# Head products of 64 contraction rows in the two halves of TensorE's array, in place of zero-padded key copies

## The chip, the cores and the metric

The kernel runs on one core of one Trainium2 chip. The metric is the time of one execution on the device in microseconds, as the median of several runs. TensorE (PE) multiplies matrices, VectorE (DVE) and ScalarE work element by element, GpSimd (POOL) does a few small operations, and the queue of SyncE (SP) issues nearly all transfers.

## The reference

The network has two layers of 256 tokens and width 1024. Each layer is a half-step feed-forward part, a mixer, and a second half-step feed-forward part. The mixer works on four groups of four heads with 64 features each, all in float32:

```python
    y_fox = merge_heads(forgetting_attention(to_heads(fq), to_heads(fk), to_heads(fv), fox_logf))
...
    h_m = mlstm_chunkwise(to_heads(mq), to_heads(mk), to_heads(mv),
...
    h_r = chunked_decay_attention(rq, rk, to_heads(rv), ret_loga)
...
    h_s = chunked_decay_attention(Ch, Bh, xh * dt[..., None], dt * A[:, None])
```

Each of the four needs, per head, the products of all queries with all keys no later than they are: a contraction over the 64 features of the head. In ssd (the last) two heads share one key group, so that there are two products instead of four.

## The kernel before

The feed-forward and projection products use pairs of float32r numbers, a high and a low part (`whi`, `wlo`), with three matmuls for each product. The weights come by transfer into `raw`; ScalarE makes the high part (L193) and DVE the low one (L194). Between them DVE works off conditioning sums (L246, `araw`) that have nothing to do with the mixer. These projection matmuls (L660 to L662 and L211 to L213) are what PE does between the steps of the mixer.

In `mixers_in`, run once for each layer, `ORDER` (L49) gives the order in which the parts are traced; a scheduler then puts each engine's instructions in a row, so that PE finds projection matmuls while a mixer waits. What stands in a row on one engine runs in that order.

Queries and keys lie with features on partitions: heads 0 and 1 in the first tile of 128 partitions, 64 each, heads 2 and 3 in the second. A product of one head should take 64 of the 128 rows. The kernel takes all 128 instead: the keys are copied into tiles of zeros (`kz[0]` for retention and later fox, `kz[1]` for mlstm, `bz` for ssd), with each head's 64 rows in their place and zeros in the others. `pad_copy` (L682) writes them in two operations of 64 partitions, from `e_rk` (L1032), `e_mk` (L1065) and `e_fk` (L1084); `e_sbc` writes `bz` in a loop. POOL clears the tiles at the stage's start (L611).

The products come in blocks, each in one PSUM bank of `bank_b`, a pool of three banks. In mlstm (`qk_ts`, L744) and fox (L960) block 0 is the first 128 queries of all four heads, 128 columns each; blocks 1 and 2 are the later 128 queries of two heads each, 256 columns a head. Retention has two blocks of two heads with 256 columns (L995) and one of four with 128 (L1000); ssd has two products of each length (L865, L866). fox adds a row sum with `add_row` (L742) into the same bank first.

Behind the products: DVE multiplies mlstm's scores and sums them in one operation per head (L939), for fox it adds the mask and takes the maximum (L964), and for retention it multiplies by `dec` (L997, L1001). mlstm and fox then transpose the weights on PE (`transpose_p`, L767 to L772; fox only after ScalarE's exponentials, L969), and `pv_tm` (L711, L713) makes the weighted sum of the values in a bank of the same pool, the numerator. `head_norm` squares it on ScalarE (L815) and sums it on DVE (L817); for the power of -0.5 the factor goes through POOL (`rsqrt`, L336 and L337). `scaled` (L1071) multiplies mlstm's numerator by the factor into `ml`; until then its bank is taken. Last, each mixer's output is transposed (`to_fm`, L693) for the output projection.

## Time and profile before

| | |
|---|---|
| median of 3 runs | 1102.37 us (1099.95 to 1106.05) |
| the profiled execution | 1099.75 us, its span 1098.0 us |
| PE, DVE, ScalarE, POOL busy | 98%, 78%, 49%, 5% of the span |
| the two mixing stages | about 212 to 347 us and 752 to 886 us |

A matmul's recorded length includes the way through the array, which overlaps the next matmul; the distance from one start to the next is what a matmul costs in a row. In a timeline a merged row gives the start of its first instruction, the time to the end of its last, and their count. A float32 product is two passes on PE, each recorded as a matmul of its own; a program's listing counts it once.

### The profile page before, as it was taken

To read this page: it belongs to the slowest core of one execution; us is meant where nothing else is said; L and a number is where in the kernel's file an instruction comes from. 1 tells how busy PE (TensorE), PEld (TensorE's weight loads), DVE (VectorE), ACT (ScalarE), POOL (GpSimd) and SP (SyncE) were. 2 spreads that over 40 slices of the span, in tenths; PEclk is the share of its full clock that TensorE was granted. 3 is DMA by queue.
4 is the path that set the end of the run, shared out by engine and by line. 5 is a ranking of instruction groups with operands and counts; after the bars stand their busy time and mean duration, and the time that the engine had idled before them with its cause. 6 is when DMAs were issued, how large, how long until landed. Compare 5 with 4: busy or idle time off the path is not lost.

```text
span 1098.0 us, 21819 instructions
## 1 busy us (share of the span) xinstructions
PE 1075.2 (98%) x8785; PEld 1058.8 (96%) x8785; DVE 859.2 (78%) x1511; ACT 538.1 (49%) x893; POOL 59.2 (5%) x76
## 2 busy tenths in 40 slices
PE   8999999999999999999999999899999999999998
PEld 6999999999999999999999999899999999999998
DVE  6899889799858988788888888886976688666541
ACT  4565434455555654334465434345545567444441
POOL 0000000200012000000100000011001120000010
PEclk9999999999999999999999999899999999999999
DMA  9889889955425688888858888884633355655531
GB/s 366 325 315 344 311 316 339 307 186 200 155 86 173 214 295 295 311 300 318 285 199 287 298 317 294 300 284 157 210 99 116 115 186 189 198 179 189 180 130 39
DMA packets 73879, 258.17 MB, mean 235 GB/s; under 512 B 10161, under 2 KB 12465, under 8 KB 73266
## 3 DMA queue, kind: packets, MB, share of 16 engines
q1 hardware_dynamic: 73490, 256.26, 67.4%
q8 instruction: 69, 1.13, 0.4%
q10 hardware_dynamic: 288, 0.52, 0.1%
q14 instruction: 32, 0.26, 0.1%
HBM read 255.70 MB, written 1.05 MB: 234 GB/s over the span
## 4 chain that ended last, share of the span: by engine, by line
PE 76%; DMA 9%; DVE 8%; issue 4%; ACT 2%; POOL 0%; SPq 0%; DVEq 0%; ACTq 0%; POOLq 0%
PE pa L212 22%; PE pa L213 22%; PE pa L211 21%; DMA araw<-in_ada_dram 7%; DVE wlo L194 3%; PE pa L660 2%; PE pa L661 2%; PE pa L662 2%; DMA raw<-in_w13a_dram 1%; ACT whi L193 1%; PE pb L711 1%; DVE ul L378 1%; DVE araw L246 1%; DMA sh<-in_ada_dram 1%; PE stat L329 1%
## 5 line engine op out<-in xcount | busy, mean ns | idle before, releaser
L193 ACT ACTIVATE whi<-raw 128x1024 fp32r<-128x1024 f32 (+1 forms) x340 | 354.3, 1046 | 270.7 <-issue 75.9
L194 DVE TENSOR_TENSOR wlo<-raw,whi 128x1024 fp32r<-128x1024 f32 (+1 forms) x340 | 411.2, 1213 | 95.7 <-ACT whi L193 95.1
L211 PE MATMUL pa<-hh,whi 128*128 128x256 f32 x1424 | 404.5, 284 | 1.3 <-ACT whi L193 1.3
L213 PE MATMUL pa<-hh,wlo 128*128 128x256 f32 x1424 | 403.2, 283 | 0.5 <-DVE wlo L194 0.5
L212 PE MATMUL pa<-hl,whi 128*128 128x256 f32 x1424 | 403.2, 283 | 0.0
L211 PEld LDWEIGHTS pa<-hh,whi 128*128 128x128 f32 x1424 | 273.2, 192 | 3.5 <-ACT whi L193 2.2
L213 PEld LDWEIGHTS pa<-hh,wlo 128*128 128x128 f32 x1424 | 273.2, 192 | 0.7 <-DVE wlo L194 0.7
L212 PEld LDWEIGHTS pa<-hl,whi 128*128 128x128 f32 x1424 | 273.2, 192 | 0.6 <-issue 0.5
L211 PE MATMUL pa<-sh,whi 128*128 128x256 f32 x704 | 200.9, 285 | 3.8 <-ACT sh L518 3.8
L212 PE MATMUL pa<-sl,whi 128*128 128x256 f32 x704 | 201.1, 286 | 3.2 <-DVE sl L519 3.2
L213 PE MATMUL pa<-sh,wlo 128*128 128x256 f32 x704 | 200.7, 285 | 0.0
L246 DVE CUSTOM_DVE_ANT_0 araw<-araw,cact 128x1024 f32<-128x1024 f32 x128 | 159.3, 1245 | 48.7 <-DMA araw<-in_ada_dram 48.0
L211 PEld LDWEIGHTS pa<-sh,whi 128*128 128x128 f32 x704 | 136.7, 194 | 4.2 <-ACT sh L518 4.2
L212 PEld LDWEIGHTS pa<-sl,whi 128*128 128x128 f32 x704 | 136.8, 194 | 3.6 <-DVE sl L519 3.6
L213 PEld LDWEIGHTS pa<-sh,wlo 128*128 128x128 f32 x704 | 136.8, 194 | 0.0
L518 ACT ACTIVATE sh<-s 128x256 fp32r<-128x256 f32 x88 | 36.1, 411 | 125.3 <-DVE s L511 121.0
L322 POOL TENSOR_TENSOR acc<-acc,sq 128x256 f32<-128x256 f32 x30 | 27.4, 912 | 694.0 <-ACT sq L320 693.7
L212 PE MATMUL pa<-ul,whi 128*128 128x258 f32 x208 | 60.1, 289 | 1.3 <-DVE ul L378 1.3
L211 PE MATMUL pa<-uh,whi 128*128 128x258 f32 x208 | 60.0, 290 | 0.9 <-ACT uh L377 0.9
L213 PE MATMUL pa<-uh,wlo 128*128 128x258 f32 x208 | 60.4, 291 | 0.0
L660 PE MATMUL pa<-whi,hh 128*128 128x256 f32 (+1 forms) x192 | 55.9, 291 | 0.0
L662 PE MATMUL pa<-whi,hl 128*128 128x256 f32 (+1 forms) x192 | 55.6, 290 | 0.0
(262 smaller groups left out, 1328.8 us busy)
## 6 DMA issues: line engine op xcount, KB each, us to landing
araw<-in_ada_dram SPq DMA_DIRECT2D x128, 512.0 KB, 5.2
raw<-in_w13b_dram SPq DMA_DIRECT2D x88, 512.0 KB, 4.6
raw<-in_w13a_dram SPq DMA_DIRECT2D x76, 512.0 KB, 5.7
raw<-in_w2a_dram SPq DMA_DIRECT2D x44, 512.0 KB, 5.2
raw<-in_w2b_dram SPq DMA_DIRECT2D x44, 512.0 KB, 4.2
raw<-in_wfm_dram SPq DMA_DIRECT2D x32, 512.0 KB, 4.8
raw<-in_wtm_dram SPq DMA_DIRECT2D x24, 512.0 KB, 4.4
raw<-in_wo_dram SPq DMA_DIRECT2D x16, 512.0 KB, 3.9
```

The source lines that it names most:

```text
L193: act.activation(out=hi, in_=raw, func=AF.Copy)
L194: dve.tensor_tensor(out=lo, in0=raw, in1=hi.bitcast(F32), op=ALU.subtract)
L211: pe.matmul(o, lhsT=wh, rhs=xh, start=first, stop=False)
L212: pe.matmul(o, lhsT=wh, rhs=xl, start=False, stop=False)
L213: pe.matmul(o, lhsT=wl, rhs=xh, start=False, stop=last)
L246: dve.tensor_tensor_reduce(out=raw, in0=raw, in1=cact, scale=0.5, scalar=0.0, op0=ALU.mult, op1=ALU.add, accum_out=cond[l][:, i:i + 1])
L322: eng.tensor_tensor(out=s.acc, in0=s.acc, in1=sq, op=ALU.add)
L329: m = pe.matmul(s.ps[:, t:t + 1], lhsT=v[:, t * P:(t + 1) * P], rhs=ones[:, 0:1], start=(x == 0 and t == 0), stop=(x == len(vs) - 1 and t ...
L518: act.activation(out=sh[:, c, :], in_=s, func=AF.Copy)
L660: pe.matmul(os[t], lhsT=h[0][:, k, ts], rhs=wh[:, y, :], start=(k == 0), stop=False)
L661: pe.matmul(os[t], lhsT=h[0][:, k, ts], rhs=wl[:, y, :], start=False, stop=False)
L662: pe.matmul(os[t], lhsT=h[1][:, k, ts], rhs=wh[:, y, :], start=False, stop=(k == KT - 1))
```

## The change

The padded tiles, their clearing and `pad_copy` are gone. The keys of retention, mlstm, fox and ssd lie in tiles of their own (`kr`, `km`, `kf`, `bt`) without zeros, each written in one operation of 128 partitions.

A new function, `products`, makes a block of all four heads: for each tile x of two heads, the head in partitions 0 to 63 into bank `os[0]` and the one in 64 to 127 into bank `os[1]`, each with 64 contraction rows. Every one is pinned behind the PE instruction traced before it. A block now takes two banks, and there are two blocks instead of three: 128 columns a head, which fill half of each bank, and 256, which fill them. For retention the 256 come first. DVE's operations go through the heads of one bank and then of the other; retention has four of them instead of three. ssd's products go to two banks, one for each key group.

```diff
@@ -605,10 +605,8 @@
 
     def mixers_in(mp, l, st, done):
         h = []
-        kz = [mp.tile([P, 4, T], F32, name=f"kz{i}") for i in range(2)]
-        bz = mp.tile([P, 2, T], F32, name="bz")
-        for t in kz + [bz]:
-            pool.memset(t, 0.0)
+        kr, km, kf = (mp.tile([P, 2, T], F32, name=f"k{i}") for i in "rmf")
+        bt = mp.tile([P, T], F32, name="bt")
         row = mp.tile([P, NC_ROW], F32, name="row")
         sp.dma_start(out=row, in_=row_in[l].partition_broadcast(P))
         dec = mp.tile([P, 4, T], F32, name="dec")
@@ -679,13 +677,6 @@
                     pool.tensor_tensor(out=v[:, t, :], in0=v[:, t, :], in1=g, op=ALU.mult)
             return v
 
-        def pad_copy(dst, fn):
-
-            for j in range(2):
-                ps = slice(64 * j, 64 * j + 64)
-                n = dst.shape[1] // 2
-                fn(dst.rearrange("p (n j) t -> p j n t", j=2)[ps, j], ps)
-
         def to_fm(y):
             o = bank_b()
             for t in range(2):
@@ -741,15 +732,22 @@
             x = rows[:, :P] if o.shape[-1] == P else rows[:, P:]
             pe.matmul(o, lhsT=selR[:, r:r + 1].to_broadcast([P, P]), rhs=x, start=first, stop=last)
 
-        def qk_ts(q, k, b, o):
-
-            n = P if b == 0 else T
-            tsl = slice(0, P) if b == 0 else slice(P, T)
-            for x, h in enumerate(heads_of(b)):
-                pe.matmul(o[:, x * n:(x + 1) * n], lhsT=q[:, h // 2, tsl], rhs=k[:, h, :n], start=True, stop=True)
-
-        def heads_of(b):
-            return list(range(4)) if b == 0 else [2 * b - 2, 2 * b - 1]
+        def products(os, a, asl, b, bsl, first=True):
+
+
+            n = bsl.stop - bsl.start
+            for x in range(2):
+                for j in range(2):
+                    ps = slice(64 * j, 64 * j + 64)
+                    tc.keep_in_program_order(pe.matmul(os[j][:, x * n:(x + 1) * n], lhsT=a[ps, x, asl], rhs=b[ps, x, bsl],
+                                                       start=first, stop=first or x == 1))
+
+        def half_heads(p, j):
+
+            return p.rearrange("p (a j) t -> p j a t", j=2)[:, j]
+
+
+        BLOCKS = ((slice(0, P), slice(0, P)), (slice(P, T), slice(0, T)))
 
         def p_tiles():
             t = hp.tile([P, KT * TS], F32, tag="u", name="pp", bufs=2)
@@ -860,16 +858,17 @@
                 for x, (oo, lt, rh) in enumerate(mm):
                     pe.matmul(oo, lhsT=lt, rhs=rh, start=(x == 0), stop=(x == len(mm) - 1))
                 act.activation(out=(e1 if b == 0 else e0[:, hs, :]).rearrange("p h t -> p (h t)"), in_=o, func=AF.Exp)
-            o0, o1 = bank_b(), bank_b()
-            for g in range(2):
-                pe.matmul(o0[:, g * T:(g + 1) * T], lhsT=bz[:, g, :P], rhs=sc, start=True, stop=True)
-                pe.matmul(o1[:, g * P:(g + 1) * P], lhsT=bz[:, g, P:], rhs=sc[:, P:], start=True, stop=True)
+            og = bank_b(), bank_b()
+            for ss, n0, n1 in (slice(0, P), 0, T), (slice(P, T), T, T + P):
+                for g in range(2):
+                    ps = slice(64 * g, 64 * g + 64)
+                    pe.matmul(og[g][:, n0:n1], lhsT=bt[ps, ss], rhs=sc[ps, ss.start:], start=True, stop=True)
             for g in range(2):
                 hs = slice(2 * g, 2 * g + 2)
                 dve.tensor_tensor(out=e0[:, hs, :], in0=e0[:, hs, :],
-                                  in1=o0[:, g * T:(g + 1) * T].unsqueeze(1).to_broadcast([P, 2, T]), op=ALU.mult)
+                                  in1=og[g][:, :T].unsqueeze(1).to_broadcast([P, 2, T]), op=ALU.mult)
                 dve.tensor_tensor(out=e1[:, hs, :], in0=e1[:, hs, :],
-                                  in1=o1[:, g * P:(g + 1) * P].unsqueeze(1).to_broadcast([P, 2, P]), op=ALU.mult)
+                                  in1=og[g][:, T:T + P].unsqueeze(1).to_broadcast([P, 2, P]), op=ALU.mult)
             ox = bank_b()
             for t in range(2):
                 for j in range(2):
...
@@ -931,14 +931,15 @@
                 act.activation(out=p0[:, h, :], in_=p0[:, h, :], func=AF.Exp, bias=nm[:, h:h + 1])
                 act.activation(out=p1[:, h, :], in_=p1[:, h, :], func=AF.Exp, bias=nm[:, 4 + h:5 + h])
             den = mp.tile([P, 8], F32, tag="den", name="den")
-            for b in range(3):
-                o = bank_b()
-                qk_ts(mq, kz[1], b, o)
-                for x, h in enumerate(heads_of(b)):
-                    pp, n, d = (p0, P, h) if b == 0 else (p1, T, 4 + h)
-                    dve.tensor_tensor_reduce(out=pp[:, h, :], in0=pp[:, h, :], in1=o[:, x * n:(x + 1) * n],
+            for b, (ts, ss) in enumerate(BLOCKS):
+                os = bank_b(), bank_b()
+                products(os, mq, ts, km, ss)
+                pp, n = (p0, p1)[b], ss.stop
+                for j, h in ((j, 2 * x + j) for j in range(2) for x in range(2)):
+                    x = h // 2
+                    dve.tensor_tensor_reduce(out=pp[:, h, :], in0=pp[:, h, :], in1=os[j][:, x * n:(x + 1) * n],
                                              scale=1.0 / 32, scalar=0.0, op0=ALU.mult, op1=ALU.add,
-                                             accum_out=den[:, d:d + 1])
+                                             accum_out=den[:, 4 * b + h:4 * b + h + 1])
             dve.scalar_tensor_tensor(out=den, in0=den, scalar=-1.0, in1=den, op0=ALU.mult, op1=ALU.max)
             dve.tensor_tensor(out=den, in0=den, in1=em, op=ALU.max)
             dve.reciprocal(out=den, in_=den)
@@ -949,19 +950,16 @@
             p0, p1 = p_tiles()
             m = mp.tile([P, 8], F32, tag="fm", name="fm")
             den = mp.tile([P, 8], F32, tag="fden", name="fden")
-            for b in range(3):
-                o = bank_b()
-                n = P if b == 0 else T
-                tsl = slice(0, P) if b == 0 else slice(P, T)
-                hs = heads_of(b)
-                for x, h in enumerate(hs):
-                    add_row(o[:, x * n:(x + 1) * n], arow, h, x == 0)
-                for x, h in enumerate(hs):
-                    pe.matmul(o[:, x * n:(x + 1) * n], lhsT=fq[:, h // 2, tsl], rhs=kz[0][:, h, :n], start=False,
-                              stop=(x == len(hs) - 1))
-                for x, h in enumerate(heads_of(b)):
-                    pp, n, d, am = (p0, P, h, amask) if b == 0 else (p1, T, 4 + h, amask1)
-                    dve.tensor_tensor_reduce(out=pp[:, h, :], in0=o[:, x * n:(x + 1) * n], in1=am, scale=1.0,
+            for b, (ts, ss) in enumerate(BLOCKS):
+                os = bank_b(), bank_b()
+                pp, n, am = (p0, p1)[b], ss.stop, (amask, amask1)[b]
+                for j in range(2):
+                    for x in range(2):
+                        add_row(os[j][:, x * n:(x + 1) * n], arow, 2 * x + j, x == 0)
+                products(os, fq, ts, kf, ss, first=False)
+                for j, h in ((j, 2 * x + j) for j in range(2) for x in range(2)):
+                    x, d = h // 2, 4 * b + h
+                    dve.tensor_tensor_reduce(out=pp[:, h, :], in0=os[j][:, x * n:(x + 1) * n], in1=am, scale=1.0,
                                              scalar=NEG, op0=ALU.add, op1=ALU.max, accum_out=m[:, d:d + 1])
             dve.tensor_scalar(out=m, in0=m, scalar1=-1.0, scalar2=None, op0=ALU.mult)
             for pp, x in ((p0, 0), (p1, 4)):
@@ -988,17 +986,12 @@
 
         def ret_front(rq, rv):
             p1, p0 = p_tiles()
-            for hb in range(2):
-                o = bank_b()
-                for x in range(2):
-                    h = 2 * hb + x
-                    pe.matmul(o[:, x * T:(x + 1) * T], lhsT=kz[0][:, h, :P], rhs=rq[:, h // 2, :], start=True, stop=True)
-                hs = slice(2 * hb, 2 * hb + 2)
-                dve.tensor_tensor(out=p0[:, hs, :], in0=o.rearrange("p (h t) -> p h t", h=2), in1=dec[:, hs, :], op=ALU.mult)
-            o = bank_b()
-            for h in range(4):
-                pe.matmul(o[:, h * P:(h + 1) * P], lhsT=kz[0][:, h, P:], rhs=rq[:, h // 2, P:], start=True, stop=True)
-            dve.tensor_tensor(out=p1, in0=o.rearrange("p (h t) -> p h t", h=4), in1=dec[:, :, :P], op=ALU.mult)
+            for p, ss in (p0, slice(0, P)), (p1, slice(P, T)):
+                os, n = (bank_b(), bank_b()), T - ss.start
+                products(os, kr, ss, rq, slice(ss.start, T))
+                for j in range(2):
+                    dve.tensor_tensor(out=half_heads(p, j), in0=os[j][:, :2 * n].rearrange("p (a t) -> p a t", a=2),
+                                      in1=half_heads(dec[:, :, :n], j), op=ALU.mult)
             num = pv_tm(p0, p1, rv)
             f = head_norm(num, "r")
             return num, f
@@ -1030,8 +1023,7 @@
             rotary(rotated("rq"), lambda r, rs: dve.tensor_tensor(out=v["rq"], in0=r, in1=rs, op=ALU.add))
 
         def e_rk():
-            rotary(rotated("rk"), lambda r, rs: pad_copy(
-                kz[0], lambda o, ps: dve.tensor_tensor(out=o, in0=r[ps], in1=rs[ps], op=ALU.add)))
+            rotary(rotated("rk"), lambda r, rs: dve.tensor_tensor(out=kr, in0=r, in1=rs, op=ALU.add))
 
         def e_sx():
             th, a = conv_silu(mp, taken("sx", "rl"), l, C_SW, C_SB, (0, 1))
@@ -1042,9 +1034,7 @@
             th, a = conv_silu(mp, taken("sbc", "ml"), l, C_SW, C_SB, (2, 3))
             v["sc"] = mp.tile([P, T], F32, tag="sc", name="sc")
             silu2(v["sc"], th[:, 1, :], a[:, 1, :])
-            for j in range(2):
-                ps = slice(64 * j, 64 * j + 64)
-                silu2(bz[ps, j, :], th[ps, 0, :], a[ps, 0, :])
+            silu2(bt, th[:, 0, :], a[:, 0, :])
 
         def e_v(name):
             v[name] = tm_evac(v["o" + name], "v")
...
```

The lines cut away are the loop headings of mlstm's row sums and the two one-line copies of `km` and `kf`.

PE in layer 0 at mlstm's products, before (`pa` rows are projection matmuls, L767 transposes for head 0):

```order
L661 MATMUL pa<-wlo,hh 128x256
L662 MATMUL pa<-whi,hl 128x256
L749 MATMUL pb<-kz_2674,mq 128x128 x4
L749 MATMUL pb<-kz_2674,mq 128x256 x4
L660 MATMUL pa<-whi,hh 128x256
L661 MATMUL pa<-wlo,hh 128x256
L662 MATMUL pa<-whi,hl 128x256
L660 MATMUL pa<-whi,hh 128x256
L661 MATMUL pa<-wlo,hh 128x256
L767 MATMUL pb<-tab,pp 128x128
```

and with the change, where L742 is the line of `products`, L765 transposes for head 0, and `pa` rows from L658 on are the projection:

```order
L659 MATMUL pa<-wlo,hh 128x256
L742 MATMUL pb<-km,mq 128x128 x4
L742 MATMUL pb<-km,mq 128x256
L660 MATMUL pa<-whi,hl 128x256
L658 MATMUL pa<-whi,hh 128x256
L742 MATMUL pb<-km,mq 128x256 x3
L765 MATMUL pb<-tab,pp 128x128
L659 MATMUL pa<-wlo,hh 128x256
L660 MATMUL pa<-whi,hl 128x256
L658 MATMUL pa<-whi,hh 128x256
```

The second block is cut into one product and three, with two projection matmuls between (three in layer 1), and five more (nine in layer 1) now stand behind the first transpose.

PE in layer 0 from retention's products (`kz_2673`) to its weighted sum (`v,pp`), before:

```order
L995 MATMUL pb<-rq,kz_2673 128x256 x3
L1000 MATMUL pb<-rq,kz_2673 128x128 x4
L661 MATMUL pa<-wlo,hh 128x256
L662 MATMUL pa<-whi,hl 128x256
L660 MATMUL pa<-whi,hh 128x256
L711 MATMUL pb<-v,pp 128x64 x5
L661 MATMUL pa<-wlo,hh 128x256
L713 MATMUL pb<-v,pp 128x64
```

and with the change, from the first product of the block of 128 columns on; ahead of it stand the three products of 256 columns and twelve projection matmuls:

```order
L742 MATMUL pb<-rq,kr 128x128
L660 MATMUL pa<-whi,hl 128x256
L658 MATMUL pa<-whi,hh 128x256
L659 MATMUL pa<-wlo,hh 128x256
L660 MATMUL pa<-whi,hl 128x256
L742 MATMUL pb<-rq,kr 128x128 x3
L658 MATMUL pa<-whi,hh 128x256
L659 MATMUL pa<-wlo,hh 128x256
L660 MATMUL pa<-whi,hl 128x256
L658 MATMUL pa<-whi,hh 128x256
L659 MATMUL pa<-wlo,hh 128x256
L702 MATMUL pb<-v,pp 128x64 x5
```

Between the end of mlstm's weighted sum and retention's there are now 21 projection matmuls, where three stood; in layer 1 there are 16. The one product of 256 columns that comes before them stands inside mlstm's weighted sum, as before.

DVE in layer 0 at retention (`pp<-pb,dec` are the copies of its scores, `hv` the norm factor, `ml` the scaled numerator of mlstm), before:

```order
L997 TENSOR_TENSOR pp<-pb,dec 128x512
L817 TENSOR_REDUCE hv<-hsq 128x8
L997 TENSOR_TENSOR pp<-pb,dec 128x512
L819 TENSOR_TENSOR hv<-hv,den 128x8
L1001 TENSOR_TENSOR pp<-pb,dec 128x512
L820 TENSOR_TENSOR hv<-hv,den 128x8
L246 ISA araw,cond_89<-araw,cact 128x1024
L246 ISA cond_89 128x1
L336 TENSOR_SCALAR hv<-hv 128x8
L823 TENSOR_TENSOR hv<-hv,den 128x8
L817 TENSOR_REDUCE hv<-hsq 128x8
L1071 TENSOR_TENSOR ml<-pb,hv 128x512
```

and with the change:

```order
L815 TENSOR_REDUCE hv<-hsq 128x8
L993 TENSOR_TENSOR pp<-pb,dec 128x2x256
L817 TENSOR_TENSOR hv<-hv,den 128x8
L993 TENSOR_TENSOR pp<-pb,dec 128x2x256
L818 TENSOR_TENSOR hv<-hv,den 128x8
L251 TENSOR_TENSOR cond_89<-cond_89,col 128x8
L336 TENSOR_SCALAR hv<-hv 128x8
L262 SCALAR_TENSOR_TENSOR cond_89<-cond_89,col 128x8
L821 TENSOR_TENSOR hv<-hv,den 128x8
L1061 TENSOR_TENSOR ml<-pb,hv 128x512
L993 TENSOR_TENSOR pp<-pb,dec 128x2x128 x2
L815 TENSOR_REDUCE hv<-hsq 128x8
```

The copies of the 128-column block have moved behind `ml`, and a conditioning sum that stood between now comes earlier.

At fox the first block (four row sums, four products) is followed by two row sums, then ten projection matmuls, and then the two other row sums and the four products of 256 columns; before, the three blocks stood one behind the other. Seventeen projection matmuls come between the last product and the first transpose, as before (sixteen in layer 1 before). ssd's four products stand together, 256 columns twice and then 128 columns twice. Between the transposes of mlstm's output and of ssd's there are 52 projection matmuls, 32 before.

## Rows read from the trace of the kernel before

**Rows 1.** The page's busy table: engine, busy us, share, instructions.

```profile
PE 1075.2 (98%) x8785; PEld 1058.8 (96%) x8785; DVE 859.2 (78%) x1511; ACT 538.1 (49%) x893; POOL 59.2 (5%) x76
```

**Rows 2.** Busy time in the first mixing stage (us from the span's start; busy, instructions, clock).

```profile
212.00:347.00 135.00, 132.38 (x1060) 128.57 (x1059) 109.42 (x258) 70.16 (x131) 13.23 (x16) 1.00 0.50 168
```

**Rows 3.** PE's timeline at ssd's products: start, length us, line, tile, count.

```profile
268.47 0.38 PE L866 MATMUL pb<-sc,bz 128*128 128x128 f32 x2
268.69 0.60 PE L865 MATMUL pb<-sc,bz 128*128 128x256 f32 x2
269.12 0.38 PE L866 MATMUL pb<-sc,bz 128*128 128x128 f32 x2
```

**Rows 4.** PE's timeline at the conditioning rows (strips of columns).

```profile
10.03 0.25 PE L329 MATMUL stat<-tab,acc 128*128 128x1 f32 x1
...
10.21 1.04 PE L268 MATMUL pb<-raw,ck 128*1 128x256 f32 x16
11.18 0.73 PE L166 MATMUL pa<-warm 128*128 128x512 f32 x2
```

**Rows 5.** The operation that writes mlstm's padded copies: ns least/median/most, first and last start.

```profile
L598 DVE SCALAR_TENSOR_TENSOR kz<-cvt,cva x4: 673/687/690, 278.1 to 816.7; 64x512 f32<-64x512 f32 x4
```

**Rows 6.** Timeline of PE and DVE at mlstm's products, layer 0.

```profile
288.00 0.28 PE L662 MATMUL pa<-whi,hl 128*128 128x256 f32 x1
288.12 2.78 PE L749 MATMUL pb<-kz,mq 128*128 128x128 f32 x16
...
287.80 2.48 DVE L194 TENSOR_TENSOR wlo<-raw,whi 128x1024 fp32r<-128x1024 f32 x2
290.19 0.28 DVE L939 CUSTOM_DVE_ANT_0 pp<-pp,pb 128x128 f32<-128x128 f32 x1
```

**Rows 7.** Timeline of PE, ScalarE and DVE at retention, layer 0; in brackets idle and releaser.

```profile
297.34 1.51 PE L995 MATMUL pb<-rq,kz 128*128 128x256 f32 x6
...
300.12 1.22 PE L711 MATMUL pb<-v,pp 128*128 128x64 f32 x10
...
297.54 0.60 ACT L815 ACTIVATE hsq<-pb 128x512 f32<-128x512 f32 x1 [2.68 <-PE pb L713]
...
298.02 0.69 DVE L997 TENSOR_TENSOR pp<-pb,dec 128x512 f32<-128x512 f32 x1 [2.88 <-PE pb L995]
298.63 0.67 DVE L817 TENSOR_REDUCE hv<-hsq 128x8 f32<-128x512 f32 x1
299.23 0.68 DVE L997 TENSOR_TENSOR pp<-pb,dec 128x512 f32<-128x512 f32 x1
...
301.79 0.17 DVE L336 TENSOR_SCALAR hv<-hv 128x8 f32<-128x8 f32 x1
303.71 0.17 DVE L823 TENSOR_TENSOR hv<-hv,den 128x8 f32<-128x8 f32 x1 [1.75 <-POOL hv L337]
...
304.39 0.68 DVE L1071 TENSOR_TENSOR ml<-pb,hv 128x512 f32<-128x512 f32 x1
```

**Rows 8.** Timeline of PE and DVE at fox, layers 0 and 1.

```profile
308.60 0.48 PE L742 MATMUL pb<-rows,selR 128*128 128x256 f32 x2
...
311.66 0.28 DVE L964 CUSTOM_DVE_ANT_0 pp<-pb,tab 128x128 f32<-128x128 f32 x1
...
848.41 0.48 PE L742 MATMUL pb<-rows,selR 128*128 128x256 f32 x2
...
849.86 0.28 DVE L964 CUSTOM_DVE_ANT_0 pp<-pb,tab 128x128 f32<-128x128 f32 x1
```

**Rows 9.** PE groups by line, transposes of fox and of ssd: idle before, releaser.

```profile
L767 PE MATMUL pb<-tab,pp 128*128 128x128 f32 x16 | 4.4, 279 | 1.9 <-ACT pp L969 1.9
...
L693 PE MATMUL pb<-tab,sy 128*128 128x128 f32 x8 | 1.5, 279 | 1.1 <-DVE sy L899 1.1
```

**Rows 10.** Busy time and granted clock in a feed-forward stage.

```profile
492.00:496.40 4.40, 1.90 (x13) 1.50 (x13) 4.38 (x8) 2.58 (x4) 0.00 (x0) 1.00 0.67 217
496.40:499.80 3.40, 3.40 (x18) 3.40 (x17) 2.07 (x3) 0.00 (x0) 0.00 (x0) 0.50 0.92 357
```

9 lines of the change are left out of this document (5 added, 4 removed).

## The prediction

> **What bounds the kernel now.** I read the page's busy table first. TensorE (PE) is busy 98% of the span, VectorE (DVE) 78%, ScalarE 49% [rows 1]: a matmul that goes away is worth its time wherever PE does not wait anyway. Then busy time by stage, because the change lies only in the two mixing stages. In the first PE is busy 132.4 of 135.0 us, at the full granted clock, with the DMA engines half idle [rows 2]; the second reads alike. So the bound of both stages is PE, and transfers don't limit them; what PE loses there, it loses in a few waits for DVE and ScalarE, which come below.
>
> **The products.** One float32 product is two passes of PE, each recorded as a matmul. In the trace two passes of 256 columns take 0.43 us and two of 128 take 0.22 us, from start to start [rows 3]: 0.216 and 0.11 us each. A layer has 14 products of each length, four for retention, mlstm and fox each and two for ssd, which makes 56 passes of each in both layers. In a row they take 56 x 0.216 + 56 x 0.11 = 18.3 us.
>
> The change keeps their number; what it can win is that a product in rows 0 to 63 and one in rows 64 to 127 run side by side. No row shows halves of rows. The nearest shows strips of columns: the 16 passes of the conditioning rows, four strips wide and 256 columns each, begin at 10.21, and the next matmul begins at 11.18 [rows 4], 0.97 us later, where one after another they would need 16 x 0.216 = 3.5 us. Four strips ran at once. The bounds for the halves are therefore full overlap and none; I take full overlap, as the strips do.
>
> Only neighbours in PE's order can pair. Per layer, ssd's two lengths take one slot each. mlstm's first block (128 columns) and both fox blocks take two slots instead of four. mlstm's second block and both retention blocks are split by the order into one product and then three, so they take three slots instead of four: one alone, two together, one alone. That makes 9 slots for 14 products of 256 columns and 8 for 14 of 128, saving 5 x 0.432 + 6 x 0.22 = 3.5 us per layer, **-7.0 us** in all.
>
> **Switching.** Each group of half-height products is an entry and an exit of that mode. In the strips, the first pass came 0.18 us after the start of the last full-height one, 0.07 more than its spacing of 0.11; the last slot ended at 10.21 + 4 x 0.216 = 11.07 and the next matmul began 0.11 us later [rows 4]. So 0.18 us a group, with nothing and 0.33 us (the 0.38 us of a pass less its spacing, twice) as ends. There are nine groups per layer (ssd 1, mlstm 2, retention 4, fox 2). Four of them (mlstm's single product, retention's two groups of 128 columns, fox's first block) stand just ahead of a wait that swallows them, which leaves 10 x 0.18 = **+1.8 us**. The Trainium skill ("TensorEngine Tiling (Array Packing)", Key Properties) says that a change of tiling mode drains TensorE, which speaks against a change that makes 36 of them. By that rule the 0.33 us would hold and the sum be 1.5 us higher; the strips' row shows about half.
>
> **Copies.** A half-height copy of 512 elements takes 0.69 us on DVE [rows 5], a full-height operation of 512, such as retention's copies below, as much. So one of each pair goes away: per layer DVE loses two such operations and one of half the length for ssd, some 1.7 us, ScalarE one copy, POOL its memsets. None stands on PE's way now; I cost it at nothing, except where it brings DVE sooner to a reduction. If DVE were already waiting there, that too would be worth nothing.
>
> **New waits.** The pool has three banks of this kind. A block now takes two half-used ones at once where it took one after another, so PE waits for DVE where it did not.
>
> mlstm, second block: its second bank is one of the first block's. Before, PE began at 288.12 and DVE's first reduction at 290.19, behind two weight splits [rows 6]; one of these, 1.2 us, now stands behind. The bank is free two reductions later, some 0.5 us, near 290.19 - 1.24 + 0.5 = 289.4; PE asks after two slots of 128, one of 256 and two projection matmuls (0.12 us each [rows 6]), at 289.2. **+0.2 us** in layer 0, nothing in layer 1.
>
> Retention: its weighted sum needs a bank, and its own scores hold two, so it must have the one in which mlstm's numerator lies until it is scaled. In DVE's new order that scaling comes after both copies of the first block and after the norm factor, which POOL raises to a power. From the end of mlstm's weighted sum at 297.34: 0.2 us to ScalarE's square and 0.60 in it, a reduction 0.60, copy 0.61, small product 0.17, copy 0.61, two small ones 0.34, the way through POOL and back 1.92 (301.79 to 303.71), a small product 0.17, the scaling 0.68: 5.9 us [rows 7], and 5.7 in layer 1, which has one small one less. PE has in between two slots of 256, three of 128 and 21 projection matmuls, 0.86 + 0.66 + 2.52 = 4.0 us; in layer 1 16 of them, 3.4 us. It waits 1.9 and 2.3 us, **+4.2 us**. Before it started the weighted sum at 300.12, while the scaling came at 304.39: another bank was free.
>
> fox, second block: PE is through the first at 308.60, DVE begins to reduce at 311.66 and frees a bank after two reductions of 0.28 us, some 0.5 us later; in layer 1 848.41 and 849.86 [rows 8]. PE has two row sums and ten projection matmuls meanwhile, 12 x 0.12 = 1.44 us. That gives 3.56 - 1.44 = 2.1 us, less about 1.2 for a conditioning sum (128x1024, as a split) that the new order takes out from ahead of it, and 1.95 - 1.44 = 0.5 us: **+1.4 us**. Everything behind on PE waits with it.
>
> **Old waits that go.** PE waits 1.9 us for the first transposes of fox and 1.1 us for ssd's [rows 9]. fox's 17 projection matmuls now stand behind a block that started later, and ssd's transposes come behind 52 matmuls instead of 32. I count both as gone, **-3.0 us**; late next is ScalarE's row of exponentials, which paces the transposes before and after.
>
> **Sum.** -7.0 + 1.8 + 0.2 + 4.2 + 1.4 - 3.0 = -2.4 us. The profiled execution took 1099.75 us (span 1098.0), which would become 1097.4. It lies 2.6 us under the median of the runs, 1102.37, from which the same step gives 1100.0 us. That is my forecast: no change that can be measured, 0.5% (5.5 us) being about what can.
>
> **Rivals.**
>
> *The waits do not come.* If a bank is free for retention's weighted sum, 4.2 us drop out: -6.6 us, 1095.8. For it speaks that DVE sheds copies and idles 2.9 us ahead of its first retention copy [rows 7]; against it, that the way through POOL has a fixed length.
>
> *The halves run one after another.* Then the saving is nil. The waits shrink, since PE arrives later: retention by 0.66 each to 1.2 + 1.6, fox by 0.44 each to 0.6, mlstm's to nothing. fox's second block comes 0.9 us later to DVE, so only some 2.0 us of old waits go. 0 + 1.8 + 2.8 + 0.6 - 2.0 = +3.2 us, 1105.6, **slower than before**; with 0.33 us a group +4.7 us, 1107.1. The point that decides is whether the second half's pass begins within hundredths of a microsecond of the first or a whole pass (0.22 us) later. For it: no row of this kernel shows halves together. Against it: the strips.
>
> *Weights are the limit.* Passes of 64 columns, in the weighted sums, come no faster: 10 of them from 300.12 take 1.22 us, up to 0.12 each [rows 7]. So a pass of 128 columns may already be as short as its weight load allows, and if loads of both halves queue, the 2.7 us saved there are lost and the waits give some 0.9 back: about -0.6 us, 1101.8. The Trainium skill ("TensorE: Matmul & The Clock Gate", LDWEIGHTS) says that a load's length goes by its columns and not by its rows, so half height would not shorten it; no run here shows two halves loading.
>
> *The clock falls.* In a feed-forward stage where PE was busy only 1.9 of 4.4 us, the granted clock then stood at 0.50, 1.2 GHz, for 3.4 us [rows 10], a loss of 1.7 us; behind the wait at fox it stayed at 1.00 [rows 2]. If retention's two waits do the same, -2.4 + 3.4 = +1.0 us, 1103.4.
>
> **How the numbers follow.** Forecast 0.50, no waits 0.18, halves in a row 0.17, weights 0.08, clock 0.07. Around the forecast I allow 3 us, for switching and for the spread of the runs (1099.95 to 1106.05). The range 1093.5 to 1106.5 takes in the first rival less that spread and the second to near its upper end. Faster by over 0.5% (under 1096.9): most of the first rival and a sixth of the forecast, 0.24. Slower by over 0.5% (over 1107.9): the second rival with the dear switch and some spread, and a little of the last, 0.09. Same: 0.67.
>
> **What would show it.** Products of unlike halves starting within 0.02 us of each other; 9 slots of 0.43 us and 8 of 0.22 us per layer; about 0.1 us extra at each entry and exit; PE waiting some 2 us for DVE's scaling of mlstm's numerator ahead of retention's weighted sum, and 0.4 to 0.9 us at fox's second row sums; the 1.7 us wait at fox's transposes gone; DVE's busy time down by about 3.5 us. I am wrong if halves follow one another by whole passes, if retention's weighted sum starts without a wait, or if the mixing stages get shorter and a later stage gives it back.

## The result and the profile after

The change made the kernel slower: 1110.74 us as the median of 10 runs (1103.39 to 1114.62), against 1103.22 us for the kernel before in 10 runs of its own (1099.24 to 1107.82). The ratio is 1.0063, with an interval of 1.0037 to 1.0088, so some 7 us were lost where 2.4 us were forecast as gained. Timed a second time (below) it came to 1.0061.

The page's busy table of the changed kernel, against [rows 1]:

```profile
PE 1078.1 (97%) x8785; PEld 1055.5 (95%) x8785; DVE 857.7 (78%) x1507; ACT 536.4 (49%) x891; POOL 56.8 (5%) x70
```

It shows almost nothing: as many matmuls as before, and PE as busy. The loss has to be looked for in the mixing stages. I measure such a stage from the start of the first rotary product to the start of the next stage's column sums. In the two layers it took 137.8 and 136.1 us before, and 140.3 and 138.2 us after (224.69 to 364.99 and 769.39 to 907.60): 4.6 us more, where the change should have saved.

What PE waited for there is read from its groups by line. The changed kernel (the columns are line, operation, tile, count, busy us, mean ns, then the idle time ahead of them and who ended it):

```profile
L733 PE MATMUL pb<-rows,selR 128*128 128x128 f32 (+1 forms) x32 | 5.6, 291 | 2.0 <-DVE rl L1061 1.1 <-DVE fm L962 0.9
L702 PE MATMUL pb<-v,pp 128*128 128x64 f32 x32 | 4.9, 276 | 1.5 <-DVE ml L1061 1.5
L859 PE MATMUL pb<-st,tabR 128*128 128x512 f32 (+1 forms) x20 | 4.8, 360 | 2.0 <-DVE st L845 2.0
...
L765 PE MATMUL pb<-tab,pp 128*128 128x128 f32 x16 | 4.4, 286 | 0.1
...
L684 PE MATMUL pb<-tab,sy 128*128 128x128 f32 x8 | 1.7, 294 | 2.0 <-DVE sy L898 2.0
```

The same view of the kernel before, as far as [rows 9] doesn't have it:

```profile
L742 PE MATMUL pb<-rows,selR 128*128 128x128 f32 (+1 forms) x32 | 5.8, 296 | 0.0
L861 PE MATMUL pb<-st,tabR 128*128 128x512 f32 (+1 forms) x20 | 4.8, 360 | 0.4 <-DVE st L847 0.4
...
L711 PE MATMUL pb<-v,pp 128*128 128x64 f32 x32 | 4.8, 271 | 0.0
```

Read top down: fox's row sums wait 2.0 us (0.0 before), retention's weighted sum 1.5 (0.0), ssd's sums of decay 2.0 (0.4), fox's transposes 0.1 (1.9), ssd's transposes 2.0 (1.1). That is 7.6 us of waiting against 3.4.

The other half of the loss is in the products. PE's timeline of the changed kernel at retention in layer 0:

```profile
300.55 0.39 PE L704 MATMUL pb<-v,pt 128*128 128x64 f32 x2
300.87 1.13 PE L742 MATMUL pb<-rq,kr 64*128 64x256 f32 x6
301.92 0.39 PE L660 MATMUL pa<-whi,hl 128*128 128x256 f32 x1
302.15 0.28 PE L658 MATMUL pa<-whi,hh 128*128 128x256 f32 x1
...
303.33 0.28 PE L659 MATMUL pa<-wlo,hh 128*128 128x256 f32 x1
303.54 0.48 PE L742 MATMUL pb<-rq,kr 64*128 64x128 f32 x2
303.96 0.39 PE L660 MATMUL pa<-whi,hl 128*128 128x256 f32 x1
304.18 0.28 PE L658 MATMUL pa<-whi,hh 128*128 128x256 f32 x1
...
305.84 0.28 PE L659 MATMUL pa<-wlo,hh 128*128 128x256 f32 x1
306.63 1.30 PE L702 MATMUL pb<-v,pp 128*128 128x64 f32 x10 [0.51 <-DVE ml L1061]
```

The halves do run side by side: three products of 256 columns (six passes) take 301.92 - 300.87 = 1.05 us, where six passes in a row need 1.30, and single passes show the second half starting 0.007 us behind the first. But three products make two slots here, a pair and one alone, and 1.05 is more than two slots of 0.432, 0.86. Around the lone product at 303.54 each step is 0.1 us too long: 0.21 from the matmul ahead (0.12 is its spacing), 0.42 for two passes of 128 columns (0.22), 0.22 behind. Counted in this way (from the matmul ahead to the second one behind, less what these take in a row), a group of half-height products mostly costs 0.3 to 0.4 us of PE beside its slots, whether it holds one product or four; ssd's costs more, 0.5 to 0.6.

Two executions of one program differ outside these stages too; what the new waits are, and what they do beyond those 4.6 us, the experiments had to say.

### The profile page after: what moved, and what is told of

It is laid out like the page before. It is cut to its first block, busy times and chain, and to the rows that moved or that the text cites. A ratio compares the mean times of both kernels' runs of the same rounds, so it can differ in the third digit from the quotient of the medians.

```text
span 1106.0 us, 21802 instructions
## 1 busy us (share of the span) xinstructions
PE 1078.1 (97%) x8785; PEld 1055.5 (95%) x8785; DVE 857.7 (78%) x1507; ACT 536.4 (49%) x891; POOL 56.8 (5%) x70
## 3 DMA queue, kind: packets, MB, share of 16 engines
HBM read 255.70 MB, written 1.05 MB: 232 GB/s over the span
## 4 chain that ended last, share of the span: by engine, by line
PE 81%; DVE 7%; issue 5%; DMA 4%; POOL 1%; ACT 0%; SPq 0%; DVEq 0%; ACTq 0%; POOLq 0%
PE pa L212 25%; PE pa L213 25%; PE pa L211 25%; DMA araw<-in_ada_dram 2%; DVE wlo L194 2%; DVE ul L378 1%; PE pb L702 1%; DMA sh<-in_ada_dram 1%; POOL hv L337 1%; DMA row<-in_row_dram 1%; PE pa L658 1%; PE pa L660 1%; PE pa L659 1%; PE stat L329 1%; PE pb L859 0%
## 5 line engine op out<-in xcount | busy, mean ns | idle before, releaser
L211 PEld LDWEIGHTS pa<-sh,whi 128*128 128x128 f32 x704 | 137.4, 195 | 6.0 <-ACT sh L518 6.0
L212 PEld LDWEIGHTS pa<-sl,whi 128*128 128x128 f32 x704 | 137.3, 195 | 2.6 <-DVE sl L519 2.6
L213 PEld LDWEIGHTS pa<-sh,wlo 128*128 128x128 f32 x704 | 137.4, 195 | 0.0
L658 PE MATMUL pa<-whi,hh 128*128 128x256 f32 (+1 forms) x192 | 56.0, 292 | 0.0
```

The lines of the kernel that those rows point to most:

```text
L211: pe.matmul(o, lhsT=wh, rhs=xh, start=first, stop=False)
L212: pe.matmul(o, lhsT=wh, rhs=xl, start=False, stop=False)
L213: pe.matmul(o, lhsT=wl, rhs=xh, start=False, stop=last)
L658: pe.matmul(os[t], lhsT=h[0][:, k, ts], rhs=wh[:, y, :], start=(k == 0), stop=False)
```

## The experiments

Stage lengths are given as layer 0 / layer 1, in us. Ratios are to the kernel before, with their interval.

**Both kernels again.** No edit.

> The kernel before, unchanged, profiled and timed again: it says how far two executions of one program lie apart, place by place. Theory A (what comes late ahead of the first mixing stage belongs to one execution): the matmuls on the mean-square column sums of the first mixing, at 214.6 us before and 215.4 after, and the first rotary product, at 221.96 and 224.69, move here too by 0.5 us or more, the time is 1100 to 1108 us and the ratio 1.00 within 0.25%. Theory B (it belongs to the change): both starts come within 0.3 us of 214.6 and 221.96. Either way ssd's tables cost 0.5 us of waiting on TensorE, not 2.0.

> The changed kernel, unchanged, profiled and timed again. Theory A: the first rotary product comes at another time than 224.69 us, since weights reach the chip at other times in each execution; theory B: within 0.3 us of it. Both: the wait of 2.0 us ahead of ssd's sums of decay in the first layer, the waits of 1.4 and 0.7 us at fox's rows and the 1.0 us ahead of ssd's transposes come again within 0.4 us each, since they follow from the order of the instructions on VectorE. Ratio 1.004 to 1.009.

Before: ratio 0.9998 (0.9967 to 1.0029), stages 138.3 / 136.1, column sums at 216.8 and the first rotary product at 227.0. After: 1.0061 (1.0037 to 1.0085), stages 140.6 / 138.2, rotary product at 224.90. So what came late ahead of the first stage belongs to an execution, not to the change (theory A): the unchanged kernel moved by 5 us. The changed kernel itself came within 0.3 us of its first profile, which its expectation had named for theory B; but its third and fourth profile (below) begin the stage at 223.30 and 222.89. The stages repeat within 0.5 us. The waits came again: 1.66 us from start to start at ssd's tables (2.04 in the first profile), 1.39 and 0.75 at fox, 1.0 at ssd's transposes.

**Two half-height sums for the rotated key.**

```diff
-rotary(rotated("rk"), lambda r, rs: dve.tensor_tensor(out=kr, in0=r, in1=rs, op=ALU.add))
+def add(r, rs):
+    for j in range(2):
+        ps = slice(64 * j, 64 * j + 64)
+        dve.tensor_tensor(out=kr[ps], in0=r[ps], in1=rs[ps], op=ALU.add)
+rotary(rotated("rk"), add)
```

> The changed kernel, but retention's rotated key is written in two half-height sums of 64 rows each, as before; its tile stays unpadded and all products stay in halves. With the one full-height sum VectorE's order had moved a conditioning sum (1.2 us) ahead of ssd's tables; with two the order up to the end of mlstm's rows is that of before. If that conditioning sum is what made ssd's tables late: TensorE waits 0.5 us there instead of 2.0, fox's new waits stay, and the time falls by 1.5 us (layer 0; layer 1 has no conditioning sums at this place), to about 1.005 of before. Rival: the tables are late for another reason (weights that arrive late), and the wait stays at 2.0 us.

The wait at ssd's tables fell to 0.4 us, the one of before; stages 138.0 / 138.2, ratio 1.0039 (1.0009 to 1.0068). DVE's timeline of the changed kernel shows what the one sum had moved:

```profile
264.14 0.42 DVE L598 SCALAR_TENSOR_TENSOR bt<-cvt,cva 128x256 f32<-128x256 f32 x1
265.96 1.23 DVE L246 CUSTOM_DVE_ANT_0 araw<-araw,cact 128x1024 f32<-128x1024 f32 x1 [1.40 <-DMA araw<-in_ada_dram]
267.11 0.08 DVE L246 DVE_READ_ACCUMULATOR2_ANT cond<- 128x1 f32 x1
267.11 1.22 DVE L194 TENSOR_TENSOR wlo<-raw,whi 128x1024 fp32r<-128x1024 f32 x1
268.25 0.28 DVE L845 TENSOR_SCALAR st<-tab,lah 128x128 fp32r<-128x128 f32 x1
```

and DVE's timeline of the kernel before at the same place:

```profile
261.84 0.42 DVE L598 SCALAR_TENSOR_TENSOR bz<-cvt,cva 64x256 f32<-64x256 f32 x1
262.81 1.23 DVE L194 TENSOR_TENSOR wlo<-raw,whi 128x1024 fp32r<-128x1024 f32 x1 [0.55 <-ACT whi L193]
263.95 0.28 DVE L847 TENSOR_SCALAR st<-tab,lah 128x128 fp32r<-128x128 f32 x1
```

A conditioning sum that nobody needs yet now stands ahead of the tables (`st`), and DVE waits 1.40 us for its transfer before it even begins. One instruction fewer on DVE moved the order, and with two sums it moves back.

**Only ssd and mlstm in halves.** Retention and fox as before.

> Only ssd and mlstm take their products in halves; retention and fox keep the padded copies and the order of their banks. If products in halves pay by themselves and what loses are the waits of retention and fox: in each layer ssd and mlstm's first block save 0.43 + 0.22 + 0.44 us and mlstm's second 0.43 us, less three entries at 0.2 us, so 0.9 us a layer, and no new wait of over 0.5 us in the mixing stages: 1.8 us under before, ratio 0.998. Rival (the groups of half height cost more than they save): ratio over 1.002 with the padded retention and fox.

Stages 136.7 / 135.8, ratio 0.9984 (0.9960 to 1.0008): as expected, though the interval holds 1. ssd's transposes wait 1.1 us as before, fox's 1.2.

**The change's order and banks, with padded full-height products.**

```diff
-lhsT=a[ps, x, asl], rhs=b[ps, x, bsl]
+lhsT=of(a, x, j)[:, asl], rhs=of(b, x, j)[:, bsl]
```

(`of` gives the padded copy of head 2x + j, or the pair's tile.)

> The changed kernel's order, banks and blocks, but with zero-padded key copies as before, so that every product is full height and nothing overlaps or switches (VectorE's order up to mlstm's rows is again that of before, so the kernel to compare with is the one with two half-height sums). Stage lengths are from the first rotary product to the column sums of the next stage; with two sums they are 138.0 and 138.1 us in the two layers. Theory S (the switch at each of nine groups per layer eats nearly all that the overlap saves): the products take 0.3 us a layer longer, stages of 137.6 to 138.8 us, time within 1 us of the kernel with two sums. Rival (the overlap pays 3.5 us a layer and waits elsewhere eat it): the stages come to 140.5 us or more.

The time agrees with theory S: ratio 1.0046 (1.0017 to 1.0075), 0.7 us from the kernel with two sums. The intervals are some 6 us wide, though, so the trace has to decide. The stages, 142.4 / 141.4, look like the rival's, until the windows are read (after the five engines' busy times come the granted clock, the DMA share and GB/s):

```profile
854.10:860.90 6.80, 6.80 (x34) 6.80 (x33) 1.55 (x3) 0.60 (x1) 1.64 (x1) 0.50 0.25 78
308.00:314.80 6.80, 6.80 (x34) 6.80 (x34) 2.88 (x7) 1.93 (x3) 2.21 (x1) 0.50 0.01 1
```

In each layer the granted clock stood at 0.50, 1.2 GHz, for 6.8 us, behind waits of 1.5 and 1.6 us (start to start) for retention's weighted sum. Half of it, 3.4 us, is lost: without it the stages are 139.0 / 138.0 (the first with 0.5 us that it lost ahead of ssd). This profile was the slowest of the kernel's ten executions, so I also take all of them: with each execution's span multiplied by its mean granted clock, which takes off what the clock cost, the mean is 1096.5 us, against 1096.1 with two sums. PE's rows say it directly: in this order the padded products of a layer take 9.3 us, hardly more than their bare slots (14 x 0.432 + 14 x 0.22 = 9.1), and the halves 9.0 to 9.2, of which 5.65 are slots. So the padded products need hardly more time than the halves, and full-height groups have next to none of the extra cost.

**Whole groups.** On top of two sums:

```diff
+if first:
+    tc.keep_in_program_order(pe.matmul(os[0][:, :4], lhsT=identR, rhs=SLR[:, :4], start=True, stop=True))
 for x in range(2):
-    for j in range(2):
+    for j in (1, 0):
```

> The kernel with two half-height sums, with a matmul of four columns that takes a block's first bank ahead of its products, so that the four products of a block wait together and run as one group: 14 groups in place of 18, none with a lone product. Theory S, with about 0.4 us lost per group: per layer two groups (0.8 us) and the lone slots (0.43 + 0.43 + 0.22 us) go, three small matmuls of 0.1 us come, so 1.5 us less, partly given back to the bank that retention's weighted sum waits for: stages of 136.7 to 137.4 us, time some 2 us under the kernel with two sums, ratio to before about 1.002. In the trace four products of 256 columns take 1.06 us and four of 128 take 0.64 us wherever they stand. Rival (the group's cost is that of its products, not of switching): the stages stay within 0.4 us of 138.

A miss: 139.4 / 137.8 (137.7 in layer 0 if the loss by 3.4 us at clock 0.50 is taken off), ratio 1.0056 (1.0033 to 1.0079). That is the rival's number, but not by its mechanism. The groups took 1.06 and 0.64 us as expected, but the time went to the next wait, in PE's groups by line:

```profile
L702 PE MATMUL pb<-v,pp 128*128 128x64 f32 x32 | 5.0, 280 | 2.7 <-DVE ml L1067 2.7
```

Retention's weighted sum waits 2.7 us where it waited 1.0 with two sums. Its bank comes free when DVE has scaled the numerator, however early PE is there: what PE saves ahead of it, it waits.

**Fox as before, mlstm's numerator copied.** Whole groups for the other three, and ahead of the square:

```diff
+num = mp.tile([P, 2, 4, 64], F32, tag="mnum", name="mnum")
+act.copy(out=num, in_=o)
```

> ssd, mlstm and retention in halves, in whole groups and with two half-height sums for the rotated key; fox as before (padded, three blocks of one bank); mlstm's numerator is copied to SBUF by ScalarE, so that its bank is free for retention's weighted sum 0.6 us after the sum is done. Theory: none of the four places that lost (ssd's tables, retention's weighted sum, fox's rows, ssd's last transposes) is later than before; the products of three mixers, 6.6 us a layer before, take 5.4 us with their entries: stages of 136.6 us in layer 0 and 134.8 in layer 1, ratio 0.997 to 0.998. Rival (each switch costs more than seen, or the copy makes ScalarE late for mlstm's square): stages no shorter than 137.8 and 136.0.

A miss as well: 137.4 / 136.5, ratio 1.0022 (1.0000 to 1.0044). The copy stands ahead of ScalarE's square and puts 0.6 us into the way to the norm factor; in layer 0 fox's third block then waits 1.23 us for the bank of retention's numerator, in layer 1 retention waits for DVE's copies (0.34 and 0.79 us).

**Only ssd and mlstm, whole groups.** The edit of the whole groups on the kernel with ssd and mlstm alone; timed twice.

> Only ssd and mlstm in halves, mlstm's second block as one group behind a matmul of four columns that takes its first bank. Against the same without it (stages 136.7 and 135.8 us, ratio 0.9984) a slot of 0.43 us goes and 0.1 to 0.2 us comes: stages of 136.4 and 135.5 us, ratio 0.998. Rival: the group waits for its second bank as long as the lone product took, and nothing is gained.

> ssd and mlstm alone in halves, mlstm's second block as one group: timed again, since the interval of the first time, 0.9956 to 1.0005, just holds 1. If the 1.4 to 1.8 us that its two mixing stages are shorter than before's (136.4 and 135.9 us against 137.8 to 138.3 and 136.1) is all there is, the ratio comes to 0.998 to 0.999; if it is the noise of the runs, to 1.000 or more.

Stages 136.4 / 135.9 both times, ratios 0.9981 (0.9956 to 1.0005) and 0.9990 (0.9958 to 1.0023). Whole groups gave 0.3 us in the first layer and nothing in the second, where 0.3 us in each was expected. It is the best version that I found, but both intervals hold 1: that it is faster than before is not shown by the times. Span times granted clock is 1092.0 us on the mean of its 24 executions, against 1093.7 us for the 114 executions of the kernel before that stand on record with their clock, so the clock aside it is 1.7 us shorter (0.9 to 2.4), as its stages are.

**The switch by itself.** In the kernel before, ahead of a chunk's first matmul, with 64 rows or with `P`:

```diff
+pe.matmul(o[:, 0, :4], lhsT=ident[:64], rhs=ident[:64, :4], start=True, stop=True)
 mm_fm(o[:, 1, :], w[0], h)
```

> The kernel before, with one more product at 73 places of the feed-forward stages, ahead of a chunk's first matmul: 64 rows high, 4 columns, float32 (two passes), its result overwritten. It measures a switch to half height and back by itself. Theory S: the stretch from the matmul ahead of it to the matmul behind it is 0.3 to 0.4 us longer than with the same product at full height; over 73 places that is 22 to 29 us in the time, less what waits for weights swallow. Rival (0.18 us, as forecast, or less): 13 us or less.

> The control: the same 73 products over all 128 rows, 4 columns. Two passes at about 0.1 us and some 0.1 us of exit: 0.3 us at each place, up to 22 us over before; the difference to the half-height one is the price of the switch alone.

1138.59 us at half height (ratio 1.0302, 1.0262 to 1.0342), 1115.89 at full height (1.0118, 1.0075 to 1.0161): 22.7 us apart, 0.31 us for each of 73 places (with three executions each; their means are 20.3 us apart, 0.28). PE's timeline at half height:

```profile
423.79 0.28 PE L213 MATMUL pa<-hh,wlo 128*128 128x256 f32 x1
424.00 0.38 PE L554 MATMUL pa<-tab 64*128 64x4 f32 x2
424.31 0.39 PE L211 MATMUL pa<-hh,whi 128*128 128x256 f32 x1
424.53 0.28 PE L212 MATMUL pa<-hl,whi 128*128 128x256 f32 x1
```

and at full height:

```profile
413.89 0.28 PE L213 MATMUL pa<-hh,wlo 128*128 128x256 f32 x1
414.02 0.28 PE L554 MATMUL pa<-tab 128*128 128x4 f32 x2
414.15 0.36 PE L211 MATMUL pa<-hh,whi 128*128 128x256 f32 x1
414.36 0.28 PE L212 MATMUL pa<-hl,whi 128*128 128x256 f32 x1
```

From the first row's start to the last's it is 0.74 us against 0.47, and the medians over all 73 places say the same: 0.209 + 0.312 + 0.222 against 0.123 + 0.138 + 0.203, 0.28 us for one switch to half height and back. The Trainium skill ("TensorEngine Tiling (Array Packing)", Key Properties) says that a change of tiling mode drains TensorE; the two traces agree that going to half height and back costs TensorE time, and give it the price. The kernel's groups cost 0.3 to 0.4 us, with passes of 128 and 256 columns in place of 4; where the other 0.1 us arises is not shown.

**Numerators kept in SBUF.** Two sums, and behind the square of mlstm and of retention:

```diff
-return num, f
+return kept(num, "rnum"), f
```

(`kept` is ScalarE's copy to a tile of its own.)

> All products in halves, the rotated key in two half-height sums, and both numerators (mlstm's and retention's) copied to SBUF by ScalarE behind its square, so that each gives its bank back some 1.2 us after its weighted sum instead of after the way through POOL. Theory (the new waits are the two numerators that hold a bank until they are scaled): the waits of 1.05 us ahead of retention's weighted sum in layer 1 and of 1.26 us at fox's second rows in layer 0 go; fox's wait of 0.5 us for its own reductions and the 1.2 us at ssd's last transposes stay: stages of 137.0 and 137.1 us against 138.0 and 138.2, ratio near 1.002. Rival (fox waits for its own reductions, as the prediction had it): fox's waits stay.

Stages 137.1 / 136.9, ratio 1.0018 (0.9995 to 1.0041), as expected. PE's groups by line:

```profile
L733 PE MATMUL pb<-rows,selR 128*128 128x128 f32 (+1 forms) x32 | 5.6, 292 | 1.2 <-DVE fm L968 1.2
...
L702 PE MATMUL pb<-v,pp 128*128 128x64 f32 x32 | 4.9, 275 | 0.0
...
L684 PE MATMUL pb<-tab,sy 128*128 128x128 f32 x8 | 1.7, 294 | 1.9 <-DVE sy L903 1.9
```

Retention's wait is gone and fox waits for its own reductions (`fm`) alone: both numerators had held a bank. The two stages together are as long as before's, 274.0 us against 273.9 (below), and the ratio's interval holds 1.

**Retention as before, its numerator kept.**

> ssd, mlstm and fox in halves; retention padded, in three blocks of one bank as before, and its numerator copied to SBUF by ScalarE. Against ssd and mlstm alone (stages 136.7 and 135.8 us): fox saves 0.3 us of products per layer net of its two switches and the old wait of 1.05 us at its transposes in layer 0, has no bank wait for a numerator, 0.5 us of wait for its own reductions, and ssd's transposes wait 0.6 us longer: 136.4 and 136.6 us, ratio 0.999. Rival (fox's two-bank blocks lose more): 138 us or more in either stage.

137.3 / 136.3, ratio 1.0009 (0.9988 to 1.0031): in layer 0 fox waits 1.3 us for its own reductions, more than the 0.5 expected, and ssd's transposes wait 2.0. In all kernels with fox in halves whose waits I read by line (after, two sums, whole groups, and the last two) that is 1.9 to 2.0 us; with fox padded beside ssd and mlstm in halves it is 1.1. But the padded control has no halves at all and waits 1.9, so it is the order that does it. DVE's and POOL's timelines of the changed kernel, ahead of these transposes (`sv` is the factor and `sy` the output of ssd, `g` a gate that POOL multiplies):

```profile
335.00 0.70 DVE L896 TENSOR_SCALAR sv<-sv 128x2 f32<-128x2 f32 x1 [0.49 <-POOL sv L337]
...
335.94 1.34 DVE L898 SCALAR_TENSOR_TENSOR sy<-sy,sv,row 128x256 f32<-128x256 f32 x2
...
334.94 0.74 POOL L677 TENSOR_TENSOR g<-g,row 128x256 f32<-128x256 f32 x1
336.10 0.90 POOL L677 TENSOR_TENSOR g<-g,row 128x256 f32<-128x256 f32 x1 [0.42 <-DVE g L598]
```

and of the kernel before:

```profile
328.75 0.17 DVE L897 TENSOR_SCALAR sv<-sv 128x2 f32<-128x2 f32 x1 [0.81 <-POOL sv L337]
...
329.97 0.87 DVE L899 SCALAR_TENSOR_TENSOR sy<-sy,sv,row 128x256 f32<-128x256 f32 x2
...
331.26 2.41 POOL L679 TENSOR_TENSOR g<-g,row 128x256 f32<-128x256 f32 x2 [2.54 <-DVE g L598]
```

The gate now comes before `sy` in DVE's order, so POOL multiplies it while DVE makes `sv` and `sy`, and DVE's small operation on `sv` takes 0.70 us in place of 0.17 and its two on `sy` 1.34 in place of 0.87, in both layers: 1.0 us more on the way to the transposes. Every kernel that waits 1.9 to 2.0 us has these longer rows in both layers, and none that waits 1.1; with fox as before and mlstm's numerator copied, `sv` alone is long, in layer 0 alone, and the waits are 0.9 and 0.6. That POOL's work is what stretches them is read from this agreement; no run moved it alone.

**The rest of the loss.** Profiles alone, no edit.

> The changed kernel, unchanged, a third profile. The two mixing stages were 140.3 and 140.6 us in the first layer and 138.2 twice in the second, 4.5 us over before together, while the runs lie some 7 us apart. Theory C (the rest is the granted clock, which in some executions also falls behind the new waits, as it did behind retention's in the padded and the grouped kernel): a stretch at clock 0.50 lies inside a mixing stage in one of the two new profiles, and that stage is 1.7 us longer for each 3.4 us of it. Theory D (the rest is the scatter of weights that arrive late in the feed-forward stages): the stages are 140 to 141 and 138.2 us again, with no such stretch behind retention or fox.

> The changed kernel, unchanged, a fourth profile; the same expectations as for the third.

> The kernel before, unchanged, a third profile: mixing stages of 137.8 to 138.3 and 136.1 us again, by either theory; what lies outside them moves by several microseconds as it did between the first two profiles (818.8 and 825.6 us).

After: 140.5 / 139.8 and 141.8 / 139.8; before: 139.6 / 136.1, with 3.4 us at clock 0.50 from 224.0, ahead of the whole change. Two windows of the fourth profile of after, at ssd's tables and behind retention's wait:

```profile
268.00:272.00 4.00, 3.81 (x12) 3.19 (x13) 3.51 (x10) 1.06 (x2) 0.00 (x0) 0.57 0.46 167
...
855.30:858.70 3.40, 3.40 (x18) 3.40 (x17) 0.86 (x2) 1.71 (x3) 0.11 (x1) 0.50 0.00 0
```

PE had waited 1.88 us for the tables, and then sat at the low clock; the third profile has the same 3.4 us from 853.1, behind retention's wait (from 849.9). Take 1.7 us off for each and the four profiles of after agree: 278.5, 278.8, 278.6 and 278.2 us for both stages. Before, they are 273.9, 273.9 and 274.0, with the third's own fall taken off, and 0.5 us in the second, whose first stage ends in a fall (0.95 us of it). So the change costs 4.6 us in every execution, and another 1.7 us for each fall of the clock behind a new wait, of which these four profiles had three.

Seven profiles don't say how much that is on the mean, but every execution has its span and its mean granted clock on record. An estimate from them: the clock takes (1 - clock) x span, and the rest, clock x span, is 1098.0 us on the mean of the 22 executions of the changed kernel and 1093.7 us on the mean of 114 of the kernel before, 4.3 us apart (3.6 to 5.0), which agrees with the stages. The clock takes 10.4 us after and 8.9 us before, 1.5 us more (0.1 to 2.9). Together that is 5.8 of the 6.1 us between the means. So theory C holds for the whole: the change costs more than 4 us of work and waits, and the rest is the clock, by a size that is just clear of nothing.

## Why the prediction was wrong

Term by term, as the prediction had them:

- **Products, -7.0.** The overlap was right: pairs 0.007 us apart, 9 slots of 0.432 and 8 of 0.22 us a layer. Four products of 128 columns took 0.64 us at fox in layer 1, two slots and 0.2 us, so loads of weights don't limit them to the pace of full height (eight passes in a row, 0.89 us).
- **Switching, +1.8.** This is the step that failed first. I read 0.18 us from the strips [rows 4] and let waits swallow 8 of 18 groups. The products of a layer with their entries and exits (without fox's wait) took 9.25 us before and 9.0 to 9.2 after: some 3.5 us over the bare slots (9 x 0.432 + 8 x 0.22 = 5.65), nearly 0.4 us for each of nine groups. Products and switching together, forecast at -5.2, came to -0.3. The 0.33 us that I had weighed for a drain and set aside was nearer (0.28 us in the traces of the control, 0.31 in its medians).
- **Copies, nothing.** The writes of the three keys on DVE fell by 3.6 us as forecast (7.0 to 3.4), but "none stands on PE's way" looked at the copies, not at what their going does to the order. It cost 1.6 us at ssd's tables, shown by the kernel with two sums. DVE as a whole was busy only 1.5 us less, because its operations at ssd's output grew by 2.0 us over both layers.
- **Retention's wait, +4.2.** The mechanism was right, the size not. Counted from the end of mlstm's weighted sum at 300.87, DVE had scaled the numerator (0.69 us from 305.79) after 5.6 us, for 5.9 forecast. But PE needed 305.96 - 300.87 = 5.1 us to get there, not 4.0: three groups lie on that way, at 0.4 us each. It waited 0.5 us there and 1.5 us over both layers. What it was spared here it had paid in switching.
- **Fox's second block, +1.4.** It came to 2.0. In layer 1 the 0.5 us for its own reductions was right (0.4); in layer 0 that wait was 0.5 for 0.9 forecast, and a releaser came that I had not looked for, the bank of retention's numerator (1.1 us), the same mechanism one mixer on.
- **mlstm, +0.2.** No wait came there, which the bounds allowed.
- **Old waits, -3.0.** Fox's 1.9 us went as forecast (0.1 is left). ssd's 1.1 became 2.0: I expected that more matmuls ahead would cover it, and looked at PE's order alone. DVE's order had moved too: its last operations for ssd now run beside POOL's on the gate and take 0.5 us longer in a layer at `sv` and 0.5 at `sy`. Without that the wait would be some 0.2 us in a layer (an estimate: each operation shortened to its length of before).

Sum as measured: -0.3 + 1.6 + 1.5 + 2.0 - 1.8 + 0.9 = +3.9 us, of the 4.6 that the stages show without the falls. Of the rivals, "the halves run one after another" fell on its mechanism, though its sum (+3.2, or +4.7 with a dear switch) met the stages by luck; "the weights are the limit" fell; "the clock falls" came true in two of four profiles, at 1.7 us each as priced, and not as an alternative to the forecast but on top of it. The range ended at 1106.5 us because I let the switch be dear only together with no overlap.

## What to carry to other kernels

Before splitting products into halves of the array, count the groups and not the products: here a group had to hold more than about 0.4 us of saved passes to pay, and scattered groups of one to four products gave back nearly all that overlap saved. Two half-used banks per block also need the pool to be free earlier, so look up what each bank waits for until it is freed, numerators that wait for a norm factor above all. And where a scheduler sets the order, compare the order at the places that wait ahead of the change too: one instruction fewer moved a transfer-bound sum in front of work that PE needed, and a gate that came earlier put POOL's work beside operations of DVE that PE waited for.

## What was not expected of the hardware

The fall of the clock is not settled by the wait ahead of it: behind the same waits (1.3 us for retention in layer 1, 1.9 us or so at the tables) the granted clock stayed at 1.00 in some executions and stood at 0.50 for 3.4 us in others. Whole stages move as well: the first rotary product of the unchanged kernel started at 221.96, 227.02 and 223.55 us in three executions (the second had stood at clock 0.50 for 6.8 us from 217.6, the third had just waited 1.9 us for ScalarE), so one profile against another says little outside the stretch that was changed, while that stretch repeated within 0.5 us. And an operation of DVE on 128x2 elements took 0.17 or 0.70 us, as POOL was idle or at work beside it.
